# One normalised fp16 copy of x for four projections of a hybrid attention and gMLP block

## The chip, the cores and the metric

The kernel runs on one core of a Trainium2 chip (the program targets one core; seven others of the chip stay idle). Its time is the device time of one execution in microseconds (us). The kernel before took 736.73 us in the median of 3 runs (736.58 to 737.26).

The engines that matter: TensorE (PE) multiplies matrices and loads its weights (PEld); VectorE (DVE) and ScalarE (ACT) do elementwise work; GpSimd (POOL) does some; SyncE (SP) issues nearly all transfers between memory and the chip's own buffers (DMA). Every engine works through its own list in order, and semaphores hold an instruction until its inputs are there.

## The reference, cut to what matters

One pre-norm residual block with 1024 tokens (t), width 1024 (d):

```python
h = rmsnorm(x, norm_gain)                                  # (1024, 1024)
z = h @ w_in                                               # 1024 -> 512+128+128+512+512+512+512+2048
q, k, v, gate_a, u_in, v_in, gate_b, g_merge = split(z)
q = axial_rope(rmsnorm(q per head, q_gain)); k = axial_rope(rmsnorm(k per head, k_gain))
attn = softmax(q k^T / 8) v * silu(gate_a)                 # 8 query heads, 2 key heads, 64 wide, no mask
y_a = attn @ w_proj_attn
vv = layernorm(gelu(v_in)); v_mix = w_spatial @ vv + b     # in chunks of 128 tokens, 8 groups
y_b = (gelu(u_in) * v_mix * silu(gate_b)) @ w_proj_gmlp
g = sigmoid(g_merge + b_merge)                             # two gates of 1024 each
y = g[0] * y_a + g[1] * y_b
out = rmsnorm(x + y @ w_out, final_gain)
```

Everything is fp32 outside. Inside, each product is made from two parts of each factor, hi*hi + hi*lo + lo*hi (three matmuls, `mm3`), so that little of fp32's precision is lost.

## The kernel before, in words

**Formats.** A factor is split into hi (the value rounded to the short format) and lo (the rest, rounded again). Most products take fp32r parts (fp32 words that the TensorE reads at a reduced precision); the scores' weights, the probabilities and values of the attention (`p16`, `vS`) and the merge gates take other forms: `p16`, `vS` and the merge gates are fp16. An fp16 factor needs a scale, so the merge gates' weights are first squared and summed, and `unit_scale` makes a power of the sum (a tiny matmul, an ACT copy, four small POOL steps).

**The stages on the TensorE**, in the order of its list:

1. k and v of the attention (`kv`, 192 matmuls of 256 columns) from the raw x times the norm's gain (`xh`, `xl`; `load_x`). The norm's 1/rms per token (`rstd`) is not applied to x. It is made from a second load of x (`xn`, `add_square`) and is put on the results afterwards.
2. `v` (the reference's `v_in`, 192 matmuls of 512 columns, `v_group`), gelu on ACT with the scale `rstd`, layer norm on DVE, and the spatial mix `sp`.
3. `q` (192 matmuls), with `head_norm` and `rope` on DVE (`q_post`), then transposes to `qT`.
4. Attention. 64 score heads `s` (4 matmuls each) alternate with 32 mixes `o` (48 small matmuls each). A head of scores takes from DVE the maximum (`nm`, L553), from ACT the exponential (L557) and the fp16 hi part (L563), from DVE the lo part (L564); then a transposing DMA brings both into the layout `T` that the mix needs. Between the heads lie 24 "fills" (L488 to L490, 24 matmuls each): the paths `u`, `ga` and `gb`, half a weight block at a time. A fill's weights are cut on ACT (hi) and POOL (lo, L118), and its result is multiplied on DVE by `rB`, the 1/rms of every token spread over the partitions.
5. `yb`, the projection of the gMLP branch. Meanwhile DVE and ACT make the forms of x for the merge gates: `x_chunk` loads x again, multiplies it by gain and 1/rms, and makes seven sums and differences of its blocks, each cut into fp16 hi and lo.
6. Merge gates `g` and the attention's projection `y`, by a scheme of seven products in place of eight (`seven`), and the merge.
7. The output projection `out`, residual and final norm.

**What sets the order.** The program is written without explicit engine order; a scheduler with a model of durations orders each engine's list when the kernel is built, from the program order and priorities. At the first score heads the program issues five heads (`ahead = 5`), two fills and the last two `q_post`, then per step two heads, one mix and the planned fills.

**Names.** `xraw`: x as loaded (transposed, 8 blocks of 128 of d by 1024 tokens); `wraw`, `rawv`: weights as loaded; `scg`, `scv`: the small scale tiles; `nm000`: maximum of the first score head (numbers: key-head pair j, token block, half); `o02`: the third mix.

Of the kernel before, what the change touches and what calls it, by code (L numbers as in the profile page):

```python
# [30 lines left out]
def hybrid_block_kernel(  # L31
# [19 lines left out]
    BUFS = {"xh": 8, "xl": 8, "T16": 4, "vS": 1, "P": 2, "p16": 2, "og": 2, "rB": 1, "gg": 6}  # L51
# [89 lines left out]
    xh, xl = [], []  # L141
# [4 lines left out]
    def load_x(dt):  # L146
        raw = t4("T16", f"xraw{dt}")
        hi = t4("xh", f"xh{dt}", F32R)
        lo = t4("xl", f"xl{dt}", F32R)
# [11 lines left out]
        xh.append(hi)  # L161
        xl.append(lo)
        return raw

    ssx = const([P, NT], "ssx")

    def add_square(tt):

        xn = t4("og", f"xn{tt}")
        nc.sync.dma_start(out=xn, in_=x[C(tt), :])  # L170
        act.activation(xn, xn, AF.Square, accum_out=ssx[:, tt:tt + 1])

    def mm3(o, ah, al, bh, bl, start, stop):
        pe.matmul(o, ah, bh, start=start, stop=False)  # L174
        pe.matmul(o, ah, bl, start=False, stop=False)  # L175
        pe.matmul(o, al, bh, start=False, stop=stop)  # L176

    kvs = [ps_s(f"kv{b}") for b in range(2)]
    kvb = [s[:, H(h)] for s in kvs for h in range(2)]
    for i in range(4):  # L180
        for j in range(2):
# [5 lines left out]
            raw = load_x(dt)  # L187
# [20 lines left out]
    def nat_weights(first, dts, between=None):  # L208
        ws = []
        for dt in dts:  # L210
            raw = load_w(first + dt // 2, dt % 2)
            if dt % 2 == 0:
                hi = t4("P" if dt < 4 else "p16", f"nh{first}{dt}", F32R)
            if dt % 4 == 0:
                lo = t8("ptr", 2, f"nl{first}{dt}")
            l = lo[:, dt % 4 // 2, H(dt % 2)]
            split(hi[:, H(dt % 2)], l, raw, NWE[dt % 2], NWL[dt % 2])
            ws.append((hi[:, H(dt % 2)], l))
            if between is not None:
                between(dt)  # L220
        return ws

    def nat_group(name, g, ws):
        sp = ps_s(f"{name}{g}")
        for dt in range(8):
            for k in range(2):
                c = C(2 * g + k)
                mm3(sp[:, H(k)], xh[dt][:, c], xl[dt][:, c], ws[dt][0], ws[dt][1], dt == 0, dt == 7)
        return sp

# [808 lines left out]
```

## Time and profile before

One execution was profiled. It took 736.99 us, 0.3 us over the median of the timed runs; its span on the core was 735.2 us, so 1.8 us lie outside the span. The mean granted TensorE clock was 0.992.

| stretch of the span (us) | what the TensorE does | read from |
|---|---|---|
| 5 to 34 | kv, with the first 13 matmuls of v among them | timeline |
| 31 to 79 | v | timeline |
| 65 to 135 | spatial mix, q, transposes | timeline |
| 135.7 to about 411 | attention and its fills | timeline |
| 387 to 443 | yb | timeline |
| 450 to 640 | merge gates and y | timeline |
| 621 to 728 | out | timeline |

| engine | busy (us) | share of the span |
|---|---|---|
| PE | 714.0 | 97% |
| DVE | 565.9 | 77% |
| PEld | 531.4 | 72% |
| ACT | 431.2 | 59% |
| POOL | 110.4 | 15% |

A matmul's duration on the page (about 0.39 us for 512 columns) is its latency through the pipeline; the next one starts earlier, so what a matmul costs in a dense stretch is the step from one start to the next. A "busy" PE of 97% therefore does not say how dense the matmuls are. The rows that the prediction uses are shown there.

### The profile page before, as it was taken

To read this page: it belongs to the slowest core of one execution; us is meant where nothing else is said; L and a number is where in the kernel's file an instruction comes from. 1 tells how busy PE (TensorE), PEld (TensorE's weight loads), DVE (VectorE), ACT (ScalarE), POOL (GpSimd) and SP (SyncE) were. 2 spreads that over 40 slices of the span, in tenths; PEclk is the share of its full clock that TensorE was granted. 3 is DMA by queue.
4 is the path that set the end of the run, shared out by engine and by line. 5 is a ranking of instruction groups with operands and counts; after the bars stand their busy time and mean duration, and the time that the engine had idled before them with its cause. 6 is when DMAs were issued, how large, how long until landed. Compare 5 with 4: busy or idle time off the path is not lost.

```text
span 735.2 us, 11836 instructions
## 1 busy us (share of the span) xinstructions
PE 714.0 (97%) x4633; PEld 531.4 (72%) x4633; DVE 565.9 (77%) x822; ACT 431.2 (59%) x770; POOL 110.4 (15%) x101
## 2 busy tenths in 40 slices
PE   8999999998999999999999996999999999999996
PEld 8978888776777788788887883465464556488885
DVE  6556868799797988878789999888887898952223
ACT  6634564685797887777784775654455536621011
POOL 0011223133132232213200003001101110000000
PEclk9999999999999999999999998999999999999999
DMA  8830301054889999998999500130121005440202
GB/s 307 317 129 1 115 16 43 1 122 94 150 157 182 176 180 167 183 170 175 154 245 287 132 30 14 45 129 15 46 98 58 0 1 184 157 146 1 114 30 86
DMA packets 152904, 85.59 MB, mean 116 GB/s; under 512 B 135440, under 2 KB 136080, under 8 KB 152848
## 3 DMA queue, kind: packets, MB, share of 16 engines
q1 hardware_dynamic: 152560, 84.56, 46.6%
q8 instruction: 36, 0.59, 0.3%
q10 hardware_dynamic: 288, 0.28, 0.1%
q14 instruction: 20, 0.16, 0.1%
HBM read 47.07 MB, written 4.19 MB: 70 GB/s over the span
## 4 chain that ended last, share of the span: by engine, by line
PE 83%; DVE 5%; ACT 5%; DMA 5%; issue 1%; POOL 1%; SPq 0%; POOLq 0%; ACTq 0%; DVEq 0%
PE o L576 5%; PE out L175 4%; DMA T<-p 4%; PE out L176 4%; PE out L174 4%; PE s L550 3%; PE s L551 3%; PE g L174 3%; PE g L175 3%; PE g L176 3%; PE gb L488 2%; PE q L174 2%; PE q L175 2%; PE v L175 2%; PE v L174 2%; PE q L176 2%
## 5 line engine op out<-in xcount | busy, mean ns | idle before, releaser
L564 DVE SCALAR_TENSOR_TENSOR p<-P,ri,p 128x1024 f16<-128x1024 f32 x64 | 83.4, 1304 | 26.4 <-ACT p L563 26.3
L557 ACT ACTIVATE P<-s,nm 128x1024 f32<-128x1024 f32 x64 | 71.2, 1113 | 24.2 <-DVE nm L553 20.8
L563 ACT ACTIVATE p<-P,ri 128x1024 f16<-128x1024 f32 x64 | 73.1, 1145 | 15.7 <-DMA T<-p 8.8
L553 DVE TENSOR_REDUCE nm<-s 128x1 f32<-128x1024 f32 x64 | 77.6, 1214 | 3.0 <-PE s L551 2.9
L576 PEld LDWEIGHTS <-vS 128*64 128x64 f16 x1536 | 45.3, 111 | 19.0 <-issue 17.8
L576 PE MATMUL o<-T,vS 128*64 128x128 f16 x1536 | 52.0, 222 | 4.2 <-DMA T<-p 3.8
L118 POOL TENSOR_TENSOR wl<-wraw,wh 128x512 fp32r<-128x512 f32 x24 | 39.9, 1665 | 97.7 <-ACT wh L112 55.6
L550 PE MATMUL s<-kT,qT 128*128 128x512 f32 x128 | 52.9, 413 | 0.0
L551 PE MATMUL s<-kT,qT 128*128 128x512 f32 x128 | 50.9, 397 | 0.0
L911 ACT ACTIVATE sq<-xr 128x1024 f32<-128x1024 f32 x7 | 7.4, 1062 | 65.4 <-DVE xr L969 65.4
L969 DVE TENSOR_TENSOR xr<-out,xr 128x1024 f32<-128x1024 f32 x7 | 8.6, 1224 | 47.6 <-PE out L176 47.5
L674 POOL TENSOR_SCALAR scg<-scg 128x1 f32<-128x1 f32 x8 | 6.5, 807 | 206.7 <-ACT scg L673 206.6
L550 PEld LDWEIGHTS s<-kT,qT 128*128 128x128 f32 x128 | 24.3, 189 | 6.3 <-issue 0.2
L551 PEld LDWEIGHTS s<-kT,qT 128*128 128x128 f32 x128 | 24.3, 190 | 5.4 <-issue 0.2
L112 ACT CAST wh<-wraw 128x512 fp32r<-128x512 f32 x35 | 21.4, 616 | 10.4 <-PE ga L489 3.4
L682 ACT ACTIVATE wg<-graw,scg 128x512 f16<-128x512 f32 x16 | 11.4, 721 | 26.6 <-PE g L176 13.2
L488 PE MATMUL ga<-xh,wh 128*128 128x512 f32 x64 | 26.0, 406 | 0.8 <-DVE ga30w L494 0.5
L488 PE MATMUL u<-xh,wh 128*128 128x512 f32 x64 | 25.8, 402 | 0.0
L488 PE MATMUL gb<-xh,wh 128*128 128x512 f32 x64 | 25.5, 399 | 0.0
L175 PE MATMUL yb<-gml,wh 128*128 128x512 f32 x64 | 25.5, 398 | 0.0
L490 PE MATMUL u<-xh,wl 128*128 128x512 f32 x64 | 25.4, 397 | 0.0
L490 PE MATMUL gb<-xh,wl 128*128 128x512 f32 x64 | 25.4, 396 | 0.0
(554 smaller groups left out, 2143.9 us busy)
## 6 DMA issues: line engine op xcount, KB each, us to landing
wraw<-in_wall_dram SPq DMA_DIRECT2D x59, 256.0 KB, 3.4
graw<-in_wall_dram SPq DMA_DIRECT2D x16, 512.0 KB, 5.8
xraw<-in_xT_dram SPq DMA_DIRECT2D x13, 512.0 KB, 6.4
xn<-in_x_dram SPq DMA_DIRECT2D x8, 512.0 KB, 6.3
wor<-in_wall_dram SPq DMA_DIRECT2D x8, 512.0 KB, 5.1
xr<-in_x_dram SPq DMA_DIRECT2D x8, 512.0 KB, 3.8
out_dram<-xr SPq DMA_DIRECT2D x7, 512.0 KB, 2.6
xraw<-in_xT_dram SPq DMA_DIRECT2D x5, 256.0 KB, 5.5
```

What stands on the lines that cost most here:

```text
L174: pe.matmul(o, ah, bh, start=start, stop=False)
L175: pe.matmul(o, ah, bl, start=False, stop=False)
L176: pe.matmul(o, al, bh, start=False, stop=stop)
L488: pe.matmul(o, wh[:, C(dt % 4)], xh[dt][:, H(h)], start=(dt == 0), stop=False)
L490: pe.matmul(o, wl[:, C(dt % 4)], xh[dt][:, H(h)], start=False, stop=(dt == 7))
L550: pe.matmul(sp[:, H(hf)], qs, kT[:, 2 * v, H(hf)], start=True, stop=False)
L551: pe.matmul(sp[:, H(hf)], qs, kT[:, 2 * v + 1, H(hf)], start=False, stop=True)
L553: dve.tensor_reduce(out=nm, in_=sp, axis=AX.X, op=ALU.max, negate=True)
L557: act.activation(Pt, sp, AF.Exp, bias=nm, accum_out=rsum)
L563: act.activation(hi, Pt, AF.Copy, scale=ri)
L564: dve.scalar_tensor_tensor(out=lo, in0=Pt, scalar=ri, in1=hi, op0=ALU.mult, op1=ALU.subtract)
L576: pe.matmul(ot[64 * h:64 * h + 64, 0:128], vS[:, kt, v, 64 * vl:64 * vl + 64], T[:, h, 8 * p + kt, :], start=(n == 0), stop=(n == len(part ...
```

## The change

It does six things:

- **x is read once.** The eight raw blocks stay on chip. Sums of squares come from them: a square of each block on ACT (POOL for two), added on DVE, then 16 matmuls with a column of ones (`sst`). The second load (`xn`) is gone; `rstd` and `rB` are made early.
- **`norm_all`** multiplies each block by gain and `rB` (DVE), casts it to fp16 (ACT) and takes the rest (DVE): `x16`, eight tiles with hi and lo.
- **v and q** are products of `x16` and of fp16 weights. Their weights are squared and summed on ACT, scaled by `unit_scale`, and cut by `split16` (ACT hi, DVE lo). `rstd` is no longer needed on the results; the weights' scale takes its place.
- **u, ga and gb**: `all_scales` loads the 24 half blocks once more, squares them and makes all 12 scales at once. `prep` loads them again and cuts them on ACT (hi) and DVE (lo; before on POOL), up to four blocks ahead of their fills. Fills are fp16; `silu2` reads the bank directly, without the product with `rB`.
- **Merge gates**: three of the seven forms of x are blocks of x itself and are taken from `x16`; four per chunk are still made.
- Buffers: new tags, so that the raw x and `x16` share ten buffers.

The core of the diff:

```diff
-    def add_square(tt):
-        xn = t4("og", f"xn{tt}")
-        nc.sync.dma_start(out=xn, in_=x[C(tt), :])
-        act.activation(xn, xn, AF.Square, accum_out=ssx[:, tt:tt + 1])
+    def add_square(dt):
+        t = t4("T16", f"xsq{dt}")
+        if dt in SQPOOL:
+            pool.tensor_tensor(out=t, in0=xraw0[dt], in1=xraw0[dt], op=ALU.mult)
+        else:
+            act.activation(t, xraw0[dt], AF.Square)
+        if dt in SQNEW:
+            ssq.append(t)
+        else:
+            dve.tensor_tensor(out=ssq[-1], in0=ssq[-1], in1=t, op=ALU.add)
+        if dt + 1 in SQNEW or dt == 7:
+            for tt in range(NT):
+                with tc.high_priority():
+                    pe.matmul(sst[:, tt:tt + 1], ssq[-1][:, C(tt)], ones[:, 0:1], start=(len(ssq) == 1 and tt == 0),
+                              stop=(dt == 7 and tt == NT - 1))
...
+    with tc.high_priority():
+        power_rstd(rstd, sst[:, 0:NT], NT, 1.0 / D)
+        dve.tensor_scalar(out=rstdh, in0=rstd, scalar1=0.5, scalar2=None, op0=ALU.mult)
+        rp = ps_s("rb")
+        for tt in range(NT):
+            pe.matmul(rp[:, C(tt)], rstdh[:, tt:tt + 1].broadcast_to([P, P]), identr.bitcast(F32), start=True, stop=True)
+        act.copy(rB, rp)
...
+    def nat_scale(raws, ss, dst, name):
+        for dt in range(8):
+            act.activation(dst[dt][:, 0, :], raws[dt], AF.Square, accum_out=ss[:, dt:dt + 1])
+        dve.tensor_reduce(out=ss[:, 0:1], in_=ss, axis=AX.X, op=ALU.add)
+        nscale.clear()
+        return unit_scale(ss, 1, name)
...
+    def norm_all():
+        def raw_part(dt):
+            dve.scalar_tensor_tensor(out=xraw0[dt], in0=xraw0[dt], scalar=gs[:, dt:dt + 1], in1=rB, op0=ALU.mult, op1=ALU.mult)
+        raw_part(0)
+        for dt in range(8):
+            if dt < 7:
+                raw_part(dt + 1)
+            t = sb.tile([P, 2, 1024], F16, tag="xr", bufs=BUFS["xr"], name=f"x16{dt}")
+            ia = act.copy(t[:, 0, :], xraw0[dt])
+            iv = dve.tensor_tensor(out=t[:, 1, :], in0=xraw0[dt], in1=t[:, 0, :], op=ALU.subtract)
...
+    def prep(k, et):
+        name = f"{k}{et}"
+        t = sb.tile([P, 2, 2, 512], F16, tag=WT[0], bufs=BUFS[WT.pop(0)], name=f"w{name}")
+        sc = wsc[name]
+        for i in range(2):
+            raw = load_w(W_TR + base[k] + et, i)
+            split16(t[:, i, 0, :], t[:, i, 1, :], raw, sc[0], "dve")
...
-    def silu2(zp, h, name):
-        w = t2(f"{name}w")
-        dve.tensor_tensor(out=w, in0=zp, in1=rB[:, H(h)], op=ALU.mult)
+    def silu2(zp, sc, name):
         t = t2(f"{name}t")
-        act.activation(t, w, AF.Tanh)
-        dve.scalar_tensor_tensor(out=t, in0=t, scalar=1.0, in1=w, op0=ALU.add, op1=ALU.mult)
+        act.activation(t, zp, AF.Tanh, scale=sc)
+        dve.scalar_tensor_tensor(out=t, in0=t, scalar=1.0, in1=zp, op0=ALU.add, op1=ALU.mult)
...
-        if h == 0:
-            ws[k, et] = [stream_w(W_TR + base[k] + et, i, *WENG) for i in range(2)]
         fill[k](et, h, ws[k, et])
```

How the lists move, at three places.

The TensorE, at the end of kv. Before (`nl`, `nh` are the weights' parts of v):

```order
L174 MATMUL kv0_89<-wh90_247,xh5_276 128x256
L175 MATMUL kv0_89<-wl90_248,xh5_276 128x256
L174 MATMUL kv1_90<-wh90_247,xh5_276 128x256
L175 MATMUL kv1_90<-wl90_248,xh5_276 128x256
L175 MATMUL v0_488<-nl00_384,xh0_95 128x512
L176 MATMUL v0_488<-nh00_383,xl0_96 128x512
L174 MATMUL v0_488<-nh00_383,xh0_95 128x512
```

Now the last rows of kv, and the first of v (each fp16 matmul now has a row of its own for its weights):

```order
L188 MATMUL kv1_93<-wh91_346,xl7_379 128x256
L186 MATMUL kv1_93<-wh91_346,xh7_378 128x256
L187 MATMUL kv1_93<-wl91_347,xh7_378 128x256
L188 MATMUL kv1_93<-wh91_346,xl7_379 128x256
L186 LDWEIGHTS x160_490
L186 MATMUL v0_483<-wv160_451,x160_490 128x512
L187 LDWEIGHTS x160_490
L187 MATMUL v0_483<-wv160_451,x160_490 128x512
```

Before, matmuls of v stood among those of kv from the fifth block of x on; now all of v stands behind all of kv.

ACT, at the same time, in the change (`ssv` collects the squares of v's weights, `wv16` are their parts):

```order
L158 ACTIVATE xh7_378<-xraw7_377,cs_67 128x1024
L265 COPY scv_475<-usv_473 128x1
L273 ACTIVATE wv160_451<-rawv0_449,scv_475 128x512 x2
L273 ACTIVATE wv161_452<-rawv0_449,scv_475 128x512 x2
L273 ACTIVATE wv162_453<-rawv1_450,scv_475 128x512 x2
L273 ACTIVATE wv163_454<-rawv1_450,scv_475 128x512 x2
L244 COPY rB_424<-rb_428 128x1024
L250 COPY kn_438<-kv0_92 128x256
L250 COPY kn_438<-kv1_93 128x256
L304 CAST x160_490<-xraw0_97 128x1024
```

Between the last block of x and the first cast of `x16` stand the eight scaled cuts of v's weights, the copy of `rB` and two copies of k.

DVE, around the first score head's maximum. Before:

```order
L341 TENSOR_TENSOR qs2_1256<-qst1_1081,qs2_1256 128x8x64
L341 TENSOR_TENSOR qs3_1273<-qst1_1081,qs3_1273 128x8x64
L311 TENSOR_REDUCE qf2_1528<-qtmp2_1526 128x16
L553 TENSOR_REDUCE nm000_1365<-s000_1360 128x1
L312 TENSOR_TENSOR qf2_1528<-qf2_1528,rsq_460 128x16
L133 TENSOR_SCALAR qf2_1528<-qf2_1528 128x16
L553 TENSOR_REDUCE nm001_1383<-s001_1378 128x1
```

Now (`wu3`, `wa1`, `wb0`: parts of fill weights):

```order
L274 SCALAR_TENSOR_TENSOR wu1_1698<-wraw151_1703,wsc0_1188,wu1_1698 128x512
L274 SCALAR_TENSOR_TENSOR wu3_2540<-wraw170_2541,wsc0_1188,wu3_2540 128x512
L274 SCALAR_TENSOR_TENSOR wu3_2540<-wraw171_2545,wsc0_1188,wu3_2540 128x512
L417 TENSOR_TENSOR qs2_1373<-qst1_1055,qs2_1373 128x8x64
L274 SCALAR_TENSOR_TENSOR wa1_2615<-wraw110_2616,wsc0_1188,wa1_2615 128x512
L274 SCALAR_TENSOR_TENSOR wa1_2615<-wraw111_2620,wsc0_1188,wa1_2615 128x512
L708 TENSOR_REDUCE nm000_1549<-s000_1544 128x1
L383 TENSOR_REDUCE qf2_1709<-qtmp2_1707 128x16
L274 SCALAR_TENSOR_TENSOR wb0_2682<-wraw180_2683,wsc0_1188,wb0_2682 128x512
L417 TENSOR_TENSOR qs3_1390<-qst1_1055,qs3_1390 128x8x64
L274 SCALAR_TENSOR_TENSOR wb0_2682<-wraw181_2687,wsc0_1188,wb0_2682 128x512
L708 TENSOR_REDUCE nm001_1567<-s001_1562 128x1
```

Fourteen cuts of fill weights stand on DVE ahead of `nm000`, and two more ahead of `nm001`; before, none did.

More of the change, by code (lines that the diff above doesn't have):

```diff
@@ L223, in nat_group @@
-    def nat_group(name, g, ws):
-        sp = ps_s(f"{name}{g}")
-        for dt in range(8):
[L226 to L229, printed above, removed]
-    wv = nat_weights(W_VIN, range(8), add_square)
-    ssp = ps_z("ssx")
-    gsq = small("gsq")
-    gs = const([P, NT], "gs")
-    act.activation(gs, gain, AF.Square, accum_out=gsq)
-    pe.matmul(ssp[:, 16:17], ones, gsq, start=True, stop=True)
@@ L262, in hybrid_block_kernel @@
-    bsp = t2("bsp")
-    nc.sync.dma_start(out=bsp, in_=cst[:, C_BSP:C_BSP + 512])
-    bterm = sb.tile([P, 4, 128], F32, tag="wraw", bufs=4, name="bterm")
-    for h in range(2):
-        pt = ps_o(f"wsum{h}")
-        pe.matmul(pt, ones, wsr[h], start=True, stop=True)
-        for t in (2 * h, 2 * h + 1):
-            for g2 in range(2):
-                rows = slice(64 * g2, 64 * g2 + 64)
-                dve.scalar_tensor_tensor(
-                    out=bterm[rows, t, :], in0=pt[rows, C(2 * (t % 2) + g2)], scalar=cs[rows, C_LNB + t:C_LNB + t + 1],
-                    in1=bsp[rows, C(t)], op0=ALU.mult, op1=ALU.add)
+    dve.tensor_tensor(out=rsq, in0=rstd, in1=rstd, op=ALU.mult)
@@ new lines, in hybrid_block_kernel, with unit_scale @@
+    nscale = []
+    def unit_scale(ss, n, name, tag="sc", bufs=3):
+        nscale.append(name)
+        pt = ps_oz(len(nscale), f"us{name}")
+        for i in range(n):
+            pe.matmul(pt[:, 0:1], mscale.broadcast_to([P, P]), ss[:, i:i + 1], start=(i == 0), stop=(i == n - 1))
+        sc = sb.tile([P, 2], F32, tag=tag, bufs=bufs, name=f"sc{name}")
+        act.copy(sc[:, 1:2], pt[:, 0:1])
+        pool.tensor_scalar(out=sc[:, 1:2], in0=sc[:, 1:2], scalar1=1.0, scalar2=1e-30, op0=ALU.mult, op1=ALU.add)
+        pool.tensor_tensor(out=sc[:, 0:1], in0=sc[:, 1:2], in1=mhalf[:, 0:1], op=ALU.pow)
+        pool.tensor_tensor(out=sc[:, 1:2], in0=sc[:, 1:2], in1=sc[:, 0:1], op=ALU.mult)
+        pool.tensor_scalar(out=sc[:, 1:2], in0=sc[:, 1:2], scalar1=gsc[:, 1:2], scalar2=1.0, op0=ALU.mult, op1=ALU.mult)
+        return sc
@@ new lines, in hybrid_block_kernel @@
+    rv = quads(("ptr", "ptr"), "rawv", F32)
+    wv16 = quads(("P", "P", "p16", "p16"), "wv16", F16)
+    ssv = nat_load(W_VIN, rv, "v")
+    with tc.high_priority():
+        scv = nat_scale(rv, ssv, wv16, "v")
+    scv2 = small("scv2")
+    dve.tensor_scalar(out=scv2, in0=scv[:, 1:2], scalar1=2.0, scalar2=None, op0=ALU.mult)
+    vsp = [ps_s(f"v{g}") for g in range(3)]
+    with tc.high_priority(), tc.manual_schedule(engines={dve.engine, act.engine}):
+        xlast = norm_all()
+    wv = [nat_split(dt, rv, wv16, scv) for dt in range(8)]
@@ L462, in hybrid_block_kernel @@
     q_post(0, qsts[0])
+    v_finish(2)
+    prep_next()
     q_group(2)
     q_post(1, qsts[1])
+    v_finish(3)
+    prep_next()
     q_group(3)
[L467 to L475 removed]
```

465 lines of the change are left out of this document (278 added, 187 removed).

## The prediction

> **What bounds the kernel now.** I read the page first, then the busy time by stretches, the waits of the TensorE, the chain of waits, and the timeline of single matmuls.
>
> ```profile
> PE 714.0 (97%) x4633; PEld 531.4 (72%) x4633; DVE 565.9 (77%) x822; ACT 431.2 (59%) x770; POOL 110.4 (15%) x101
> PE 83%; DVE 5%; ACT 5%; DMA 5%; issue 1%; POOL 1%; SPq 0%; POOLq 0%; ACTq 0%; DVEq 0%
> ```
>
> The TensorE carries 83% of the chain that ended last, so a cheaper matmul pays at once wherever nothing else is late. How nearly the others are late is seen by stretch (PE, PEld, DVE, ACT, POOL busy, with counts; granted clock):
>
> ```profile
> 5.50:37.00 31.50, 30.74 (x225) 28.95 (x224) 19.68 (x32) 22.45 (x37) 0.99 (x1) 1.00 0.93 339
> 37.00:138.00 101.00, 101.00 (x505) 84.35 (x504) 72.70 (x136) 49.94 (x82) 20.35 (x15) 1.00 0.17 55
> 138.00:176.00 38.00, 36.60 (x255) 28.93 (x254) 36.07 (x49) 27.88 (x57) 13.80 (x7) 1.00 0.44 91
> 240.00:280.00 40.00, 40.00 (x413) 32.44 (x408) 35.78 (x47) 34.25 (x66) 12.34 (x8) 1.00 0.94 183
> 443.70:453.00 9.30, 3.10 (x9) 1.12 (x10) 7.55 (x10) 5.02 (x10) 6.64 (x8) 0.64 0.00 0
> ```
>
> From 37 to 138 us the TensorE never stops and DVE has 101 - 72.7 = 28.3 us to spare. From 138 to 176, the first score heads, DVE is busy 36.07 of 38 us: there it is DVE that sets the pace. In the body of the attention DVE has about 4 us in 40 left. At 443.7 the TensorE stands, and the clock falls.
>
> ```profile
> PE g L174 <- ACT wg L682: 6.2, 1, 6.2
> PE o L576 <- DMA T<-p: 3.8, 3, 3.1
> 174.48 1.20 DVE p L564
> 175.70 4.24 DMA T<-p
> 179.98 1.57 PE o L576 x26
> 443.73 0.94 ACT gk L112
> 444.83 3.56 POOL scg L674
> 448.75 0.57 POOL scg L675
> ```
>
> The first two rows are the two large waits of the TensorE (total, times, longest); the others are pieces of the chain (start, length). The mix at 179.98 had to wait for DVE's lo part and the transposing DMA behind it: a DVE queue, seen from the TensorE. The wait of `g` is for a scale, through ACT and POOL.
>
> **What a matmul costs.** Starts in a v stretch, in a u fill, in a gate stretch:
>
> ```profile
> 48.06 0.40 PE L174 MATMUL v<-nh,xh 128*128 128x512 f32 x1
> 50.11 0.39 PE L174 MATMUL v<-nh,xh 128*128 128x512 f32 x1
> 241.03 0.50 PE L488 MATMUL u<-xh,wh 128*128 128x512 f32 x1
> 241.37 0.39 PE L489 MATMUL u<-xl,wh 128*128 128x512 f32 x1
> 244.34 0.40 PE L490 MATMUL u<-xh,wl 128*128 128x512 f32 x1
> 519.85 0.38 PE L174 MATMUL g<-xfT,wg 128*128 128x512 f16 x1
> 521.58 0.38 PE L176 MATMUL g<-xfT,wg 128*128 128x512 f16 x1
> ```
>
> v: 9 steps in 2.05 us, 228 ns. u: 13 steps from 241.37 in 2.97 us, 228 ns. fp16: 8 steps in 1.73 us, 216 ns. So one matmul gains 12 ns, not a factor. v and q: 384 x 12 ns = 4.6 us. Fills: 24 x 24 = 576 x 12 ns = 6.9 us. Behind a mix the first fp32r step took 0.34 us (241.03 to 241.37), 0.11 over the usual: an fp32r weight load that cannot be hidden. With fp16 weights I let that fall away at the 24 fills, 24 x 0.11 = 2.6 us; its bounds are 0 and 5 (both sides of a mix). The TensorE's gain is then 4.6 + 6.9 + 2.6 = 14.1 us, if nothing else is late.
>
> The Trainium skill, "TensorE: Matmul & The Clock Gate", section "Back-to-back issue gap", gives about 131 ns per matmul of 512 columns in a stream of weight loads and matmuls; by that figure the 960 matmuls would gain 960 x 97 ns = 93 us. The trace disagrees: the gate stretch is such a stream, and its step is 216 ns.
>
> **What DVE, ACT and POOL are given.** Prices:
>
> ```profile
> L839 DVE TENSOR_TENSOR y<-y,ga 128x1024 f32<-128x1024 f32 x8 | 9.7, 1216 | 0.0
> L683 DVE SCALAR_TENSOR_TENSOR wg<-graw,scg,wg 128x512 f16<-128x512 f32 x16 | 11.9, 747 | 3.8 <-ACT wg L682 3.2
> L118 DVE TENSOR_TENSOR xfT<-xraw,xfT 128x512 f16<-128x512 f32 x18 | 12.0, 684 | 0.0
> L118 POOL TENSOR_TENSOR wl<-wraw,wh 128x512 fp32r<-128x512 f32 x24 | 39.9, 1665 | 97.7 <-ACT wh L112 55.6
> L682 ACT ACTIVATE wg<-graw,scg 128x512 f16<-128x512 f32 x16 | 11.4, 721 | 26.6 <-PE g L176 13.2
> L816 ACT ACTIVATE gsq<-graw 128x512 f32<-128x512 f32 x32 | 19.1, 598 | 1.2 <-DMA graw<-in_wall_dram 0.7
> L134 POOL TENSOR_TENSOR rstd<-rstd,mhalf 128x8 f32<-128x8 f32 x1 | 2.0, 2027 | 33.0 <-DVE rstd L133 33.0
> L674 POOL TENSOR_SCALAR scg<-scg 128x1 f32<-128x1 f32 x8 | 6.5, 807 | 206.7 <-ACT scg L673 206.6
> ```
>
> DVE, ahead of the first score head: 6 sums of squares and 16 operations of `norm_all` at 1.216 us (26.8 us), 14 cuts of fill weights at 0.747 (10.5); v's and q's 16 cuts become scaled, 0.06 each (1); eight small `dg` fall away (2.2) and parts of `head_norm` (about 2). In all about +34 us, of which the sums of squares (7.3) lie under kv, where DVE idles 12 us; +27 us fall into the stretch that had 28.3 us to spare. From `nm000` to the lo part that released `o02`, the list holds 6 us more: the cuts at `nm001` and `wb2` (4 x 0.747 = 3.0), and pieces of `q_post` that used to be done before `nm000`. The remaining 6 cuts lie in the body, and the dropped products with `rB` (16 x 0.68 = 11 us) more than pay for them: no cost there, the TensorE's 40 us per 40 us cover it; without that cover 6 x 0.747 = 4.5 us. POOL loses 39.9 us that nobody waited for: worth nothing. ACT gains some 37 us ahead of the first exponential (squares of 40 half blocks at 0.598, casts), against 50 us spare in the 101.
>
> **Start of v.** The rows for ACT's work and for a kv matmul:
>
> ```profile
> L158 ACT ACTIVATE xh<-xraw,cs 128x512 fp32r<-128x512 f32 (+2 forms) x12 | 10.2, 866 | 5.3 <-DMA xraw<-in_xT_dram 3.7 <-DMA cs<-in_cst_dram 1.3
> L171 ACT ACTIVATE xn<-xn 128x1024 f32<-128x1024 f32 x8 | 8.5, 1064 | 4.4 <-DMA xn<-in_x_dram 4.2
> 18.04 0.28 PE L175 MATMUL kv<-wl,xh 128*128 128x256 f32 x1
> 18.88 0.28 PE L176 MATMUL kv<-wh,xl 128*128 128x256 f32 x1
> ```
>
> A kv matmul takes 0.12 us (7 steps in 0.84). Before, 13 matmuls of v stood among kv, and v ran on as if it had begun at 30.7 us. Now v needs `x16`, and that needs all of x. By the list: from about 4 us on ACT has the splits of x (10.2 us), six squares of x (1.06 each), some casts of kv's weights (2) and the eight squares of v's weights (0.6 and 0.2 to read the sum) ahead of it, 25 us, so the last `xh` comes at about 29 us; the TensorE waits for v's summed squares to 28.7 and then has some 60 kv matmuls (7.3), `wsum` (0.9) and `rb` (1.7) left: kv ends near 38.6. Meanwhile POOL does `rstd` (2.0) and the scale (0.8 + 0.75) to about 34.3; ACT then cuts v's weights, 8 x 0.63 (0.721 less the 0.09 by which neighbours overlap), to 39.4, copies `rB` to 40.4; DVE multiplies the first block to 41.6; ACT casts to 42.6; DVE takes the rest behind the second block and two copies of v, 44.6. So the TensorE idles from 38.6 to 42.6 and again to 44.6, and the clock falls, as it did at 443.7; that cost there 7 matmuls in 2.96 us in place of 1.51, 1.45 us:
>
> ```profile
> 450.51 0.63 PE L175 MATMUL g<-xf,wg 128*128 128x512 f16 x1
> 453.07 0.41 PE L174 MATMUL g<-xfT,wg 128*128 128x512 f16 x1
> ```
>
> v then runs as if begun at about 45.7: +15 us. Bounds: +9 if everything from `rB` on is there when kv ends (39.7), +19 if ACT and DVE are each 4 us later than the list's sum. I take +15, since ACT's list is in order and full.
>
> The same page of the Trainium skill, section "HAM oscillation — how this bites in real kernels", says that a wait longer than about 3.4 us halves the clock until the TensorE has been busy again; the trace agrees (0.64 over the 9.3 us quoted). By it a gap of 4 us may just miss or just meet such a window; the sum would be 1.5 us lower where it is missed.
>
> Up to the first score head the TensorE has, besides 4.6 us, also `wsum` and `rb` no longer ahead of it (2 us): +15 - 6.6 = +8.4, `s000` at 135.7 + 8.4 = 144.1. DVE must keep up with that: 27 us more in a stretch that is 6 us longer, and 28.3 us spare, so about 7 us remain for all its waits for others, where it had 28.3. I add nothing for it, and keep 0 to +8 for the range.
>
> **The first heads.** The first score and its maximum:
>
> ```profile
> 135.68 0.79 PE L550 MATMUL s<-kT,qT 128*128 128x512 f32 x1
> 137.81 1.22 DVE nm L553
> ```
>
> Before, `o02` began 179.98 - 135.68 = 44.3 us behind `s000`: 2.1 to `nm000`, 37.9 of DVE's list (137.81 to 175.68, nearly without a stop), 4.24 for the DMA. The TensorE's own work in between, its list at the steps above, is 37.1 us, so 7.2 were lost. Now DVE's part is 6 us longer, the interval 50.2; the TensorE, whose work there falls to 34.4 (q's rest is done sooner, fills are shorter), loses 15.8. `o02` begins at 144.1 + 50.2 = 194.3, 14.3 later than before. Bounds of the interval: 44.3 (what DVE is given is made up elsewhere in its list) and 53.
>
> **Behind `o02`.** The TensorE saves 21 of 24 fills' 6.9 (6.0) and the step behind mixes (2.3). The stall at `g`: DVE and ACT come freer to it (12 casts and 12 rests fewer, 12 x 0.68 = 8 us of DVE), but the last y copy, the two `gk` casts, then the scale through POOL and `wg` still follow each other: 1.0 + 1.9 + 0.2 + 1.6 + 0.7 = 5.4 us against 7.2 from the last `yb`, so -1.8. Bounds: 0 and -6 (the scale done early). Transposes, scores, out and the tail are as they were.
>
> **The sum.** 736.99 + 14.3 - 6.0 - 2.3 - 1.8 = 741.2; the profiled run was 0.3 over the median, so 740.9, and rounded down, since both DVE sums leave out that a later DVE waits less for others: **740 us**.
>
> **Rivals.**
>
> 1. *The TensorE sets the pace throughout.* `x16` is there when kv ends (+9), the first heads' interval stays at 44.3 less nothing: +9 - 6.6 = +2.4 at `s000`, the same at `o02`, then -6.0 - 2.3 - 1.8: 729. With the scale at `g` early too, 725. For it: 28.3 us spare on DVE and 50 on ACT, and a DVE that is 77% busy on the whole. Against it: 36.07 of 38 us in the first heads.
> 2. *About no change*: the gap at v is half as long as I reckon (+12), the interval 48: 737 - 1.
> 3. *DVE's waits stay.* A single mechanism: between 37 and 138 us DVE's 28.3 spare us are waits for others (powers on POOL, ACT's casts, gelu), which a fuller queue does not fill because its list is in order. From more than about 7 us of such waits on they go whole into `nm000`, and from there into `o02`. If 17 of them remain, that is 10 more: 750. Its first signs were to be seen before:
>
> ```profile
> DVE st L283 <- ACT vst L367: 5.5, 1, 5.5
> DVE qf L314 <- POOL qf L134: 3.5, 2, 3.0
> ```
>
> That is 9.0 us in three waits; against it, the first arose because gelu waited for the TensorE, and DVE will now be later itself.
>
> **How the numbers follow.** Chances: forecast 0.43 (736.5 to 746), rival 1 0.30 (721 to 733), rival 2 0.13, rival 3 0.14 (746 to 756). The range 725 to 752 leaves out about one in ten at each end at most. Differences under 0.2% (1.5 us) count as no change, about what a measurement of this kernel can tell. Slower: nearly all of the forecast and of rival 3, and a little of rival 2, 0.53; faster: rival 1 and some of rival 2, 0.34; same 0.13.
>
> **What would show it.** In the profile after: the step of v, q and the fills (216 ns); a wait of the TensorE for `x16` (ACT or DVE) of 4 to 6 us near 40 us, with the clock below 1; `s000` near 144; DVE over 93% busy from 45 us to `o02`; `o02` near 194 with a DMA wait that ends behind L719; no product with `rB` in the body, and a TensorE without gaps there; a wait of `g` of 4 to 6 us. If `s000` begins before 139, the start of v is wrong; if DVE has 10% idle in the first heads and `o02` still comes late, the DVE step is wrong; if the step of the fills is not 216, all gains are.

## The result and the profile after

The changed kernel takes 756.26 us in the median, the kernel before 736.98 beside it: a ratio of 1.0256 (95% interval 1.0234 to 1.0277), 19.3 us slower. Slower was forecast, but 3 us, and the time lies outside the range. The profiled execution took 756.27 us with a span of 754.5.

| | before | forecast | after |
|---|---|---|---|
| first score head begins | 135.7 | 144.1 | 153.4 |
| from there to the third mix | 44.3 | 50.2 | 49.1 |
| third mix to the end of the span | 555.2 | 545.1 | 552.0 |

So 17.8 of the 19.3 us are there before the attention begins. From the page after:

```profile
PE 712.2 (94%) x4683; PEld 452.2 (60%) x4683; DVE 591.6 (78%) x841; ACT 459.4 (61%) x838; POOL 80.4 (11%) x88
PE 55%; DVE 17%; ACT 13%; DMA 9%; issue 4%; POOL 1%; SPq 0%; POOLq 0%; ACTq 0%; DVEq 0%
```

The TensorE is busy 1.8 us less in a span that is 19.3 us longer, and its share of the chain of waits fell from 83% to 55%: DVE, ACT and transfers make up 39%. Its six largest waits (total, times, longest):

```profile
PE s L705 <- ACT P L712: 5.3, 5, 1.9
PE o L731 <- DMA T<-p: 5.0, 5, 1.7
PE kv L187 <- DVE wl L118: 3.7, 1, 3.7
PE usg L263 <- ACT gsq L964: 3.3, 2, 3.0
PE s L705 <- ACT qT L427: 3.2, 1, 3.2
PE q L186 <- ACT qst L544: 2.5, 2, 2.0
```

Only the second was among the large ones before. By stretch (columns as in the prediction):

```profile
5.50:37.00 31.50, 25.46 (x185) 24.56 (x185) 23.01 (x28) 21.69 (x38) 7.72 (x7) 0.89 0.88 329
37.00:50.00 13.00, 10.07 (x72) 7.94 (x71) 12.35 (x17) 10.07 (x16) 0.33 (x2) 1.00 0.00 1
80.00:120.00 40.00, 36.74 (x184) 18.80 (x183) 35.14 (x75) 31.08 (x67) 8.51 (x9) 0.96 0.38 124
170.00:200.00 30.00, 26.58 (x205) 14.88 (x204) 29.22 (x40) 22.56 (x45) 6.88 (x3) 1.00 0.59 111
```

In the first row, kv, the TensorE issued 185 matmuls where it had issued 225 before, at a clock of 0.89: the first loss, and one that the prediction did not have. In the second it stands for 3 us until `x16` is there, with DVE full. In the third it stops twice in q (1.3 us for k's lo part, 2.0 for `qst`) and its clock falls again. In the fourth DVE is busy 29.2 of 30 us.

**Inside kv.** Rows of DVE, POOL and the TensorE (start, length):

```profile
14.41 2.33 POOL L169 TENSOR_TENSOR xsq<-xraw 128x1024 f32<-128x1024 f32 x1 [2.13 <-DVE xsq L175]
14.99 1.78 DVE L200 TENSOR_SCALAR gs<-cs,gsc 128x8 f32<-128x8 f32 x1
16.68 1.21 DVE L175 TENSOR_TENSOR xsq<-xsq,xsq 128x1024 f32<-128x1024 f32 x1
17.82 0.68 DVE L118 TENSOR_TENSOR wl<-wraw,wh 128x512 fp32r<-128x512 f32 x1
18.56 0.58 PE L187 MATMUL kv<-wl,xh 128*128 128x256 f32 x1 [3.74 <-DVE wl L118]
18.94 0.41 PE L188 MATMUL kv<-wh,xl 128*128 128x256 f32 x1
19.15 0.41 PE L186 MATMUL kv<-wh,xh 128*128 128x256 f32 x1
```

The TensorE needs the lo part of kv's weights (`wl`). On DVE it is queued behind a sum of squares, and that behind an operation on 8 columns that took 1.78 us (more on it at the end). Behind the stop of 3.7 us the matmuls begin 0.21 us apart, where 0.12 was their step in the kernel before, and the stretch's clock is 0.89. kv ended at 44.7 us, not at 38.6.

**Between v and the first score head** the chain of waits runs, from 90 to 108 us, through the second load of the fills' weights:

```profile
90.27 4.12 DMA wraw<-in_wall_dram
99.22 3.12 DMA wraw<-in_wall_dram
103.18 3.55 DMA wraw<-in_wall_dram
107.09 0.73 ACT wraw L574 x2
```

ACT waits for these loads in the order of its list, to square what they bring; the copies of q's result and of the spatial mix stand behind the squares in its list, and the TensorE waits for those (2.5 us for `qst`, 1.1 for `vm`).

### The profile page after: what moved, and what is told of

It reads as the page before. It is cut to its first block, busy times and chain, and to the rows that moved or that the text cites. A ratio compares the mean times of both kernels' runs of the same rounds, so it can differ in the third digit from the quotient of the medians.

```text
span 754.5 us, 12012 instructions
## 1 busy us (share of the span) xinstructions
PE 712.2 (94%) x4683; PEld 452.2 (60%) x4683; DVE 591.6 (78%) x841; ACT 459.4 (61%) x838; POOL 80.4 (11%) x88
## 4 chain that ended last, share of the span: by engine, by line
PE 55%; DVE 17%; ACT 13%; DMA 9%; issue 4%; POOL 1%; SPq 0%; POOLq 0%; ACTq 0%; DVEq 0%
DMA T<-p 4%; DMA wraw<-in_wall_dram 4%; PE out L187 4%; PE out L188 4%; PE out L186 4%; DVE p L719 4%; PE g L186 3%; PE g L187 3%; PE g L188 3%; DVE nm L708 3%; ACT P L712 3%; ACT p L718 2%; PE o L731 2%; PE yb L186 2%; PE yb L187 2%
## 5 line engine op out<-in xcount | busy, mean ns | idle before, releaser
L705 PE MATMUL s<-kT,qT 128*128 128x512 f32 x128 | 56.2, 439 | 8.5 <-ACT P L712 5.3
L706 PE MATMUL s<-kT,qT 128*128 128x512 f32 x128 | 50.4, 394 | 0.0
L186 PE MATMUL g<-x,wg 128*128 128x512 f16 x96 | 37.4, 389 | 0.5 <-ACT wg L273 0.5
L187 PE MATMUL g<-x,wg 128*128 128x512 f16 x96 | 37.4, 389 | 0.0
L188 PE MATMUL g<-x,wg 128*128 128x512 f16 x96 | 36.9, 385 | 0.0
L186 PE MATMUL q<-wq,x 128*128 128x512 f16 x64 | 25.0, 391 | 3.6 <-ACT qst L544 2.5
L186 PE MATMUL v<-wv,x 128*128 128x512 f16 x64 | 24.3, 379 | 1.5 <-ACT x L304 1.4
L186 PE MATMUL yb<-gmh,wh 128*128 128x512 f32 x64 | 25.6, 402 | 0.0
L188 PE MATMUL v<-wv,x 128*128 128x512 f16 x64 | 23.9, 379 | 1.5 <-DVE x L305 1.5
L188 PE MATMUL out<-wo,yhl 128*128 128x512 f32 x64 | 25.4, 396 | 0.0
```

The costliest lines, as they stand in the source:

```text
L705: pe.matmul(sp[:, H(hf)], qs, kT[:, 2 * v, H(hf)], start=True, stop=False)
L706: pe.matmul(sp[:, H(hf)], qs, kT[:, 2 * v + 1, H(hf)], start=False, stop=True)
```

## The experiments

Times are medians; the kernel before, run beside each, lay at 736.5 to 737.4. The last three columns are from the timelines of the profiled executions: start of the first score head, start of the last `yb` matmul, and the stretch between, which holds the whole attention. A profiled execution is not always near the median: it lies 2.3 to 2.8 us above it in k4, k18, k5, k19 and k28, and 3.2 below it in k21.

| variant | us | score head | last yb | stretch |
|---|---|---|---|---|
| before | 736.98 | 135.7 | 442.3 | 306.6 |
| the change | 756.26 | 153.4 | 460.7 | 307.3 |
| k1 few squares | 752.88 | 148.2 | 458.6 | 310.4 |
| k2 fixed scales, fills | 751.42 | 150.9 | 455.7 | 304.8 |
| k3 fixed scales, v and q | 753.19 | 147.3 | 457.3 | 310.0 |
| k8 all three | 738.12 | 136.6 | 442.8 | 306.2 |
| k6 fills' lo on POOL | 758.76 | 151.3 | 461.6 | 310.3 |
| k22 four parts undone | 760.99 | 165.4 | 465.5 | 300.1 |
| k21 before with fp16 parts | 727.65 | 128.4 | 434.3 | 305.9 |
| k4, k18 before, 48 matmuls less | 734.31, 727.99 | 135.8, 135.3 | 441.3, 435.5 | 305.5, 300.2 |
| k5, k19 change, 48 matmuls less | 744.98, 745.01 | 151.2, 151.5 | 452.9, 453.0 | 301.7, 301.5 |
| k20 before, half transposes | 731.62 | 135.1 | 442.6 | 307.5 |
| k12 k4 with half transposes | 722.40 | 135.4 | 430.8 | 295.4 |
| k11 k4 with half maxima | 724.74 | 135.0 | 433.2 | 298.2 |
| k24, k23 one warm-up matmul less | 737.48, 755.20 | 135.7, 150.9 | 443.6, 459.8 | 307.9, 308.9 |
| k27, k28 gate scales first | 735.13, 747.47 | 135.7, 151.6 | 444.4, 463.3 | 308.7, 311.7 |

### What the start costs

Three parts of the change, each taken out alone, then together.

```diff
-            if dt > 0:
-                add_square(dt - 1)
-            if dt == 7:
-                add_square(7)
+            if dt in (1, 5):
+                add_square(dt - 1)          # k1: blocks 0 and 4 only, no sum on DVE
```

> The changed kernel with the sums of squares cut down: only blocks 0 and 4 of x are squared, and the six sums on DVE and the other six squares are left out (the 1/rms then stands for a quarter of x, so this leaves out part of the computation). Theory A (the TensorE stood in kv because the weights' lo parts were queued on DVE behind the sums of squares, and what is lost there is lost for good): kv ends near 38 us in place of 44.7, the first score head comes 5 to 8 us sooner, time 748 to 751 against 756.3. Theory B (DVE's whole list up to the first mixes decides, whatever its order): 7.3 us less DVE work, of which half shows, 752 to 754. Theory C (the start is off the path, the pace is set in the attention): 755.5 to 757.

```diff
-                act.activation(raw, raw, AF.Square, accum_out=ss[:, i, h:h + 1])    # with its 24 loads
+        dve.memset(s0, 2.0 ** 10.5)         # k2: fixed scales of the fills
+        dve.memset(s1, 2.0 ** -10.5)
```

> The changed kernel with fixed scales for the fills' weights (a power of two from the weights' spread) in place of measured ones: the second load of 24 half blocks, 24 squares on ACT and the scale's chain are left out; DVE keeps all its cuts. Theory A (between v and the first score head ACT waits in order for these loads, and k's transposes and the spatial mix wait behind it): the first score head 4 to 6 us sooner than 153.4, time 750 to 752. Theory B (DVE's amount of work decides): DVE has the same work, 755.5 to 757.

```diff
-            act.activation(dst[dt][:, 0, :], raws[dt], AF.Square, accum_out=ss[:, dt:dt + 1])
-        return unit_scale(ss, 1, name)
+        dve.memset(sc[:, 0:1], 2.0 ** 9.5)  # k3: fixed scales of v and q
+        dve.memset(sc[:, 1:2], 2.0 ** -9.5)
```

> The changed kernel with fixed scales for the weights of v and q: 16 squares on ACT and two scale chains are left out. Theory A (the start of v waits for ACT's in-order list: squares, scale through the TensorE and POOL, then eight cuts, then the copy of rB): the TensorE does not wait for the summed squares, v starts 3 to 5 us sooner, and ACT is freer later, time 750 to 753. Theory B (DVE's amount decides): no DVE work falls away, 755.5 to 757.

Measured: k1 -3.4, k2 -4.8, k3 -3.1 us. Each shows, none as much as its place in the chain suggested. k1's time is theory B's, though kv and the score head moved as theory A had it; k2's time is theory A's; k3's lies 0.2 above theory A's range. k1 took kv's end from 44.7 to 36.0 and the first score head from 153.4 to 148.2: 8.7 us won, 5.2 kept. In between, v stood 5.0 us for `x16` and 5.0 more for its own gelu on ACT (`vst`), which stood behind squares of the fills' weights and the cuts of q's:

```profile
PE v L186 <- ACT vst L440: 5.0, 1, 5.0
```

In k2 v stood 3.0 us for the same `vst`, and the gain is not at the score head (2.5, which k23 below gives by order alone) but behind it: the last matmul of the third mix began 43.5 us after the first score head in place of 50.4, with 16 of the 24 lo parts of the fills' weights cut ahead of the score head in place of 12. At the last `yb`, 2.5 of these us were left.

> The changed kernel with three cuts at once: only blocks 0 and 4 of x squared, without the six sums on DVE (the 1/rms stands for a quarter of x), and fixed scales for the weights of the fills and of v and q. Alone these gave -3.4, -4.8 and -3.1 us. Theory A (three losses one after the other, each lost for good): they add up, 743 to 747. Theory B (they are one loss seen three times: DVE's list with the normalised copy of x and the fills' cuts ahead of the first score head gates all of them): little beyond the largest, 749 to 752. If all of the loss lay in these three, 736 or less would be seen.

Together they give -18.1, more than the sum of 11.3 and more than either theory said; theory B falls. The ratio to before is 1.0015 (1.0002 to 1.0029). The three stand side by side: with one gone, another holds v or the first mixes, as ACT did in k1. What is left, the normalised copy itself, still shows. In k8, between 37 and 136 us:

```profile
37.00:136.00 99.00, 96.70 (x507) 51.39 (x506) 90.19 (x162) 56.40 (x88) 14.96 (x11) 1.00 0.16 51
```

DVE is busy 90.2 us of 99, where it had 72.7 of 101 before; v and q are cheaper for the TensorE, yet the score head begins 0.9 us later than before.

Two variants put work back where it had been. k6 cuts the fills' lo parts on POOL:

```diff
-            split16(t[:, i, 0, :], t[:, i, 1, :], raw, sc[0], "dve")
+            act.activation(raw, raw, AF.Copy, scale=sc[0])
+            act.copy(t[:, i, 0, :], raw)
+            pool.tensor_tensor(out=t[:, i, 1, :], in0=raw, in1=t[:, i, 0, :], op=ALU.subtract)
```

> The changed kernel with the lo parts of the fills' weights cut on POOL again (ACT scales the raw weights in place, casts them, POOL subtracts): DVE has 24 x 0.747 = 18 us less, 10.5 of them ahead of the first score head and 3 up to the third mix; ACT has 24 casts of 0.62 us more. Theory A (the prediction's: DVE's list gates the first score head and the mixes): 3 to 8 us less, 748 to 753. Theory B (ACT's list gates them, through the squares and cuts that stand in order): no gain or a loss, 756 to 762.

758.76: no gain, theory B. Between 150 and 200 us DVE is busy 40.9 us of 50, where it was busy 46.4 in the change, and yet nothing is won: the first score head came no earlier than order alone brings it, and the TensorE did less in those 50 us (38.7 for 42.6). ACT has 24 more casts in its list, and it held the transposed q (the wait that was 3.2 us in the change). The largest waits of the TensorE in k6:

```profile
PE s L707 <- ACT qT L427: 6.2, 1, 6.2
PE kv L187 <- DVE wl L118: 4.3, 1, 4.3
```

The columns of the stretch are those of the prediction; first the change, then k6:

```profile
150.00:200.00 50.00, 42.64 (x291) 24.63 (x290) 46.36 (x64) 36.93 (x75) 9.78 (x4) 1.00 0.48 109
```

```profile
150.00:200.00 50.00, 38.66 (x219) 21.55 (x218) 40.93 (x48) 39.91 (x79) 24.08 (x15) 0.90 0.43 109
```

So it is not DVE's amount of work alone that gates the first heads; ACT's list does it as well. (Over the whole kernel DVE's busy time fell by 6.3 us only, though 24 rests of about 0.75 us, 18 us, left it. Others took longer: the 16 products of `rope` on 128x256 elements 0.65 us each, 0.42 in the change. So k6 slowed parts of DVE's own work too, and is no clean test of its amount.)

k22 undid four parts: sums of squares from a second load, fixed scales, fills' lo on POOL with unscaled weights.

```diff
-            act.activation(t, xraw0[dt], AF.Square)
+        xn = t4("T16", f"xn{tt}")           # k22: x loaded again for the squares
+        nc.sync.dma_start(out=xn, in_=x[C(tt), :])
+        act.activation(xn, xn, AF.Square, accum_out=ssx[:, tt:tt + 1])
```

> The changed kernel with four parts of it undone: sums of squares from a second load of x as before (no DVE sums), fixed scales for the weights of v, q and the fills, and the fills' lo parts cut on POOL as before. The normalised fp16 copy of x and the fp16 products stay. Theory A (the cuts of the fills' weights on DVE ahead of the first score head and in the first mixes cost some 6 us on top of what the three-part variant at 738.1 left out): 731 to 736. Theory B (the copy of x itself, 20 us of DVE ahead of v, is what holds the start): 737 to 743, since rstd comes later from the second load.

760.99, beyond theory B's 743:

```profile
PE rb L227 <- DVE rstdh L224: 15.9, 1, 15.9
```

Half of the second load, four blocks of eight, came behind weights of v and q in the queue, `rstd` with it, and v, which now needs `rstd` before its first matmul, began at 55 us. Before, a late `rstd` cost nothing, because it was put on the results. That dependence is what the change bought with `x16`.

### fp16 without the copy

k21 is the kernel before with the parts of x and of the weights in fp16, unscaled, and nothing else:

```diff
-        hi = t4("xh", f"xh{dt}", F32R)
-        lo = t4("xl", f"xl{dt}", F32R)
+        hi = t4("xh", f"xh{dt}", F16, (P, 2048))[:, 0:1024]
+        lo = t4("xl", f"xl{dt}", F16, (P, 2048))[:, 0:1024]
```

> The kernel before with one thing changed: the parts of x (times the gain, not normalised) and of the weights of kv, v, q and the fills are fp16 in place of fp32r. No normalised copy of x, no measured scale (weights unscaled), 1/rms on the results as before, merge gates as before; every cut stays on its engine. 1152 matmuls take the fp16 form. Theory A (fp16 itself pays, and the change lost it by what it put ahead of v and of the first score head): v, q, kv about -7 us at the first score head, a part of the fills' 7 to 9, 724 to 732. Theory B (behind the first score heads the chain of the score heads gives everything back): only the part ahead of the score heads shows up to the first mixes, which wait for DVE, 733 to 737.

727.65 us, ratio 0.9867 (0.9834 to 0.9900): faster than both kernels by 9 and 29 us, and in theory A's range. Its first score head begins 7.3 us earlier than before, as theory A had it, with the TensorE never idle and DVE busy 74.9 us of 99 (72.7 of 101 before):

```profile
37.00:136.00 99.00, 99.00 (x520) 54.17 (x519) 74.92 (x142) 53.44 (x89) 23.18 (x16) 1.00 0.17 57
```

The other half of theory A did not come: the attention's stretch is 305.9 against 306.6, though its 576 fill matmuls step at 0.216 us. (The profiled execution, 724.45 us, is another 4.6 us shorter behind the last `yb`. There the TensorE's stop ahead of the merge gates is 0.2 us in place of 7.8; more on it below.)

### Where a cheaper fill goes

The TensorE was busy all the time in the body of the attention before. Leaving out fill matmuls shows what that is worth: the last two of the eight matmuls with the weights' lo part in each of the 24 fills, 48 matmuls or 10.9 us.

```diff
-            pe.matmul(o, wl[:, C(dt % 4)], xh[dt][:, H(h)], start=False, stop=(dt == 7))
+            if dt < 6:                      # k4 (k18: dt > 1); k5 and k19 the same on the change
+                pe.matmul(o, wl[:, C(dt % 4)], xh[dt][:, H(h)], start=False, stop=False)
```

> The kernel before with 48 of its 576 fill matmuls left out (the last two of the weights' lo parts in each of the 24 fills; part of the product is missing): 48 x 0.228 = 10.9 us less for the TensorE, 46 of them behind the first score heads, nothing else changed. Theory A (the TensorE sets the pace in the attention, so a faster fill pays in full, and the change lost its gain elsewhere): 726 to 727.5 against 737. Theory B (the score heads' chain through DVE, ACT and the transposing DMA is nearly as slow as the TensorE there, so most of a faster fill is lost in new waits): 731 to 736.

> The kernel before with 48 other fill matmuls left out (the first two of the weights' lo parts in each fill, not the last two): the same 10.9 us of TensorE work less. Theory A (the next limit behind the TensorE takes all but 2.5 us of it, whatever the order of the lists): 733 to 736, as with the last two (734.3). Theory B (how the scheduler happened to order the lists decides): anywhere from 726 to 737, more than 3 us from 734.3.

> The changed kernel with 48 of its 576 fill matmuls left out (48 x 0.216 = 10.4 us of TensorE work). Theory A (behind the first mixes another limit paces the attention, as in the kernel before): -0.5 to -3 us, 753 to 756. Theory B (the TensorE paces it): 746 to 748.

> The changed kernel with the first two of the weights' lo parts in each fill left out (48 matmuls, 10.4 us), not the last two, which gave 745.0. Theory A (in the changed kernel the TensorE paces the attention again): 744 to 748. Theory B (the order of the lists decides how much of it shows): more than 3 us away from 745, up to 756.

Before, -2.5 us and, for the same amount of other matmuls, -8.5; in the change -11.3 and -11.3. In the kernel before, then, an equal cut is worth 2.5 or 8.5 by the order in which the scheduler puts the lists (theory B of k4 and of k18). In the change the time falls by as much as the TensorE saves (theory B of k5, a little beyond its range, and theory A of k19). But some 2 us of that are an earlier score head, which order alone gives (k23 below), and in the profiled executions the stretch itself is 5.6 and 5.8 us shorter, of 10.4; that all of it comes from the cut is not shown. The stretch from 240 to 360 us of the kernel before, k4, k18, k11, k12 and the change, last three columns clock, mean busy share of the 16 DMA engines, GB/s:

```profile
240.00:360.00 120.00, 120.00 (x1209) 96.94 (x1204) 100.91 (x130) 95.25 (x177) 34.49 (x22) 1.00 0.95 174
```

```profile
240.00:360.00 120.00, 114.64 (x1226) 91.06 (x1225) 103.92 (x133) 97.88 (x182) 28.94 (x20) 1.00 1.00 181
```

```profile
240.00:360.00 120.00, 119.37 (x1209) 95.50 (x1208) 103.08 (x133) 98.00 (x183) 35.20 (x22) 1.00 1.00 177
```

```profile
240.00:360.00 120.00, 119.12 (x1219) 95.46 (x1214) 89.28 (x132) 97.48 (x181) 30.03 (x21) 1.00 1.01 181
```

```profile
240.00:360.00 120.00, 119.67 (x1293) 95.67 (x1292) 110.16 (x140) 103.74 (x193) 30.12 (x19) 1.00 0.55 110
```

```profile
240.00:360.00 120.00, 117.05 (x1216) 73.24 (x1215) 104.48 (x132) 94.91 (x175) 12.90 (x9) 1.00 0.87 164
```

Before, the TensorE is full and the DMA engines, busy with the transposes, are at 0.95. With a lighter TensorE (k4) they are at 1.00, and the TensorE idles 5.4 us in 120. That the full DMA engines hold it does not follow: in k18 and k11 they are at 1.00 and 1.01, and the TensorE is busy 119 us of 120. k12 halves the transposes beside it, k20 halves them alone, k11 relieves DVE beside it:

```diff
-        nc.sync.dma_start_transpose(T16[j, qt][:, h], p16)
+        nc.sync.dma_start_transpose(T16[j, qt][:, h, 0:8], hi)      # k12, k20
-        dve.tensor_reduce(out=nm, in_=sp, axis=AX.X, op=ALU.max, negate=True)
+        dve.tensor_reduce(out=nm, in_=sp[:, H(0)], axis=AX.X, op=ALU.max, negate=True)      # k11
```

> The kernel before with only the hi half of the probabilities transposed (64 DMAs of half the size; the mix reads hi in place of lo), the fills whole. Theory A (the transposing DMA is a limit only once the TensorE is relieved): the wait at the first mixes and the wait at the merge gates shrink, 726 to 733, and the attention behind the third mix stays within 2 us of its 227. Theory B (it is a limit already): the attention behind the third mix shortens by more than 5 us, 718 to 726.

> The kernel before with 48 fill matmuls left out, and only the hi half of the probabilities transposed (each of the 64 transposing DMAs moves half; the mix reads hi in place of lo, which leaves lo's share out). Theory A (DVE is the next limit behind the TensorE): only the wait at the first mixes shrinks by about 2 us, 731 to 734. Theory B (the transposing DMA, with 94% of the DMA engines' time between 240 and 360 us, is the next limit): 721 to 728.

> The kernel before with 48 fill matmuls left out (that alone gave 734.3, -2.5 us of 10.9), and the score heads' maximum taken over 512 of 1024 columns, so that DVE has 64 x 0.53 = 34 us less in the attention (the scores are scaled down by 50 so that the exponential stays finite; part of the maximum is left out). Theory A (behind the TensorE, DVE is the next limit in the attention): the 8 us that were not gained come free, and with the faster first heads more, 718 to 727. Theory B (the transposing DMA is the next limit): 731 to 734.

The stretch of the attention: half transposes alone 307.5 (no gain, theory A of k20), fewer matmuls alone 305.5 or 300.2, with half transposes 295.4 (theory B of k12, the DMA), with half maxima 298.2 (theory A of k11, DVE), against 306.6. Relieving either lets the cut pay more than in k4, so a second limit stands close behind the TensorE, and a head's chain, which goes through both, fits that. Which of the two holds more is not shown: 295.4 and 298.2 lie 4.8 and 2.0 under k18's 300.2, and order alone moves this stretch by as much (k4 against k18, 5.3). The stop ahead of the gates is gone in k20, k12 and k11; behind the last `yb` their profiled executions are 5.3, 2.7 and 4.9 us shorter than before, which is not what their edits were made for.

### What order alone does

Every edit makes the scheduler order the lists anew, so I measured that by itself: one warm-up matmul less.

```diff
-    NWARM = 10
+    NWARM = 9                               # k24 on the kernel before, k23 on the change
```

> The kernel before with 9 in place of 10 warm-up matmuls ahead of the first transfer: no work that matters falls away, but the scheduler orders some hundred rows of each list differently. Theory A (the order of the lists is worth little, and what limits the attention are the engines): 735.5 to 738. Theory B (order alone moves the time by several us, and differences of that size between variants aren't the edits'): more than 3 us away from 736.7, either way.

> The changed kernel with 9 in place of 10 warm-up matmuls. Theory A (order is worth little): 755 to 758. Theory B (order alone moves the time): more than 3 us away from 756.3, either way; the time of the first score head and the stretch behind the third mix then show which part of the 19.5 us is the change's and which the order's.

+0.1 and -1.1 us, theory A; but the change's first score head moved by 2.5 us (to 150.9, as in k5, k19, k6 and k28). Differences under 3 us between variants are therefore not read as the edits', and 6 us are possible in the attention (k4 against k18). k1 and k3 (3.4 and 3.1 us) lie barely above that, k8 (18.1) far above it.

The stop ahead of the merge gates, 7.8 us before and 6.0 after, is the second place. There the first gate's scale stands on ACT behind the last copy of y and one or two casts; a priority puts it ahead.

```diff
-        sc = unit_scale(ss, 4, f"g{dt}")
+        with tc.high_priority():
+            sc = unit_scale(ss, 4, f"g{dt}")
```

> The kernel before, where the steps that make a merge gate's scale (a tiny matmul, a copy on ACT, four steps on POOL) are given a higher priority, so that for the first gate they stand ahead of the last three copies of yb and of the casts of the attention's forms. The work is the same. Theory A (the wait of the first gate is the order of ACT's list): the wait of 6.2 us goes, 729 to 731.5. Theory B (it is the weights' or the forms' work that is late, and another wait takes its place): 734 to 737.

> The changed kernel with the same priority for the gates' scales. Theory A (order of ACT's list): the TensorE's stop of 6 us ahead of the gates goes, 750 to 752; the distance to the kernel before with the same priority stays near 19 to 20 us, so the loss of the change has nothing to do with the gates. Theory B (another wait takes its place): 754 to 757.

Before: 735.13, ratio 0.9968 (0.9957 to 0.9979). The wait of `g` is gone, and more than half of it comes back in another place, in theory B's range:

```profile
PE usg L671 <- ACT gsq L816: 3.9, 2, 3.5
```

In the change: 747.47, 8.8 us less, below the range of either theory, so there it was worth more than the wait itself. The distance to the kernel before with the same edit is 12.3 us and not 19 to 20, so some 7 us of the change's loss hang on the order of the lists ahead of the gates as well. How much of k21's 9 us is this stop can only be said roughly: between 2 us (what k27 gained) and 4.6 (what k21's profiled execution is shorter there).

## Why the prediction was wrong, step by step

**Start of v, the step that failed.** It reckoned kv's end at 38.6, v as if begun at 45.7 and the first score head at 144.1. Measured: 44.7; v's last matmul starts at 91.0, which with 192 x 0.216 is as if begun at 49.5; 153.4. Of the 9.3 us that were missed, 3.8 are there when v begins: kv's end came 6.1 later than reckoned, and the gap behind it was 2.3 shorter. The prediction had put the six sums of squares "under kv where DVE idles 12 us"; but idle time of an in-order engine is no room for work that stands ahead of what another engine waits for, and these sums stood ahead of `wl`. k1 shows that sums and squares held kv (it ends at 36.0 without six of each). It does not separate them: the operation on 8 columns took 0.21 us there too.

**"I add nothing for it."** The other 5.5 us lie between v and the score head, for which the sum had a bound of 0 to +8 for DVE's waits and took 0. By the chain of waits, what held there was ACT, in order behind the second load of the fills' weights: the prediction counted ACT's 37 us against 50 spare and so passed over their order. k2 took those loads out and gained 4.8 us, but only 2.5 at the score head, so for these 5.5 us this is read from the chain and not shown by a run. That squares, scales and sums together make nearly the whole loss (18.1 of 19.3 us) is shown by k8.

**The first heads** were right in size: 49.1 against 50.2, where before it was 44.3. The reason was half right, so part of that is luck. DVE was full there (29.2 of 30), but k6 shows that a DVE relieved of the 24 rests gains nothing when ACT has more to do for it.

**Behind the third mix** 10.1 us of gain were forecast and 3.2 came. The step of a matmul was as forecast: 0.216 us in the fills, and 0.226 behind a mix, where it was 0.34. The gates' stop was as forecast too (-1.8). What was mis-sized is the worth of a faster fill. It was taken in full because the TensorE never paused there before. k21 has the same faster fills without the copy and gained 0.7 us in the stretch, and k4 and k18 gained 1.1 and 6.4 of 10.9: in the kernel before a second limit lies some 2% behind the first at most. In the change the TensorE lost 5.3 us to the exponentials' banks and 2.2 to the transposes behind the third mix instead. That these waits come from the cuts on DVE is likely and not shown: k6 moved too much else, and k22, with the cuts on POOL and no more work for ACT at the fills, has 300.1 us in the stretch against k8's 306.2, about what order alone can do.

**The rivals.** DVE's waits that stay (750, chance 0.14) came nearest in time, but its mechanism was DVE waiting for others; here the TensorE waited for DVE and ACT. TensorE-paced throughout (729) was shown by no variant: k21's 727.65 is near its time, but by an earlier score head, and its attention gained next to nothing.

**The rule on the clock.** The prediction cited the Trainium skill, "TensorE: Matmul & The Clock Gate", section "HAM oscillation — how this bites in real kernels", for a gap at v. The stop came in kv instead (3.7 us): the slow step of 0.21 us followed it, and that agrees with the page; that the clock fell because of the stop was not tested by itself. The length of a stop alone does not decide it here: behind a stop of 2.0 us in q of the change, six matmuls on, eight steps took 0.43 us, and behind one of 3.5 us ahead of v in k3 the steps were 0.216 from the start.

## What to carry to other kernels

Normalising an operand ahead of a product, rather than its result, moves a statistic over all of the input in front of the first matmul; count what each engine's list holds ahead of that point, in order, and not how idle the engine is on the whole. Before pricing a faster engine in full, look at the next busiest resource in the same stretch (here DMA engines at 0.95 beside a full TensorE), and relieve both in one run to see whether they are two limits. Do it for two orders of the lists, since order alone moved this attention by 5 us. Try the cheap format alone first: here fp16 parts without a copy and without scales gave 9 us (2 to 5 of them perhaps the stop ahead of the gates), and with all that was built around them the kernel took 29 more. Whether unscaled parts suit other inputs was not tested.

## What the runs showed that was not expected

- A DVE operation on 128x8 elements took 1.78 us while POOL squared a 128x1024 block (14.41 to 16.74 us) and ended as that ended; the same operation took 0.22 us in the kernel before. The Trainium skill, "SBUF — State Buffer", section "SBUF: two separate sides", says that DVE and GpSimd share a port pair, which for some kinds of DVE operations one of the two holds for a whole instruction while the other blocks; this row agrees. In the seven other runs of the change in which the operation met a square on POOL it took 1.78 to 1.79 us; in k1, k8 and k22, where it came ahead of it or there was none, 0.20 to 0.21. The POOL squares were not taken out alone.
- With 64 transposing DMAs of 128x2048 fp16 in the attention the DMA engines were busy 0.95 of the time from 240 to 360 us, and 0.55 with the transposes halved beside fewer matmuls (k12); yet a share of 1.00 left the TensorE busy 119 us of 120 in k18. A full share alone did not name the limit.
- A saving can pay more together than apart (18.1 against 11.3), and a wait that is removed can return in good part (k27) or bring more than itself (k28: 8.8 for 6.0).
